# Rotary scores with a zero-padded key on all 128 rows of the array, and the latents' transposes taken up behind later steps

## The chip, the cores and the metric

The kernel runs on one core of one Trainium2 chip. The metric is the time of one execution in microseconds (us) on the device. Three runs of the kernel before gave 1155.67, 1158.75 and 1169.34 us; their median is 1158.75 us. All rows of a profile come from one further execution, which took 1158.37 us, with a span of 1156.6 us from its first to its last instruction.

The engines are named as the profile names them: PE is the matrix engine, PEld its weight loads, DVE the vector engine, ACT the scalar engine, POOL the general engine, SP the one whose queue issues nearly all transfers.

## The reference, cut to what matters

A trunk of two layers on 256 rows of width 2048 in float32. Layer 0 is a chunked gMLP. Then one shared key/value path and one attention layer with 16 heads:

```python
c_kv, k_r = jnp.split(h_kv @ w_dkv, [512], axis=-1)      # 512 latent, 64 rotary
c_kv = rms_norm(c_kv, g_kva)
kv = (c_kv @ w_ukv).reshape(B, S, 16, 128 + 128)         # key, value of each head
k_rope = apply_rope(rms_norm(k_r, g_kr), cos, sin)       # one key of 64 for all heads
c_q, z = jnp.split(h @ w_in, [512], axis=-1)
q = (rms_norm(c_q, g_qa) @ w_uq).reshape(B, S, 16, 128 + 64)
s = einsum('bqhd,bkhd->bhqk', q_nope, k_nope) + einsum('bqhr,bkr->bhqk', q_rope, k_rope)
o = softmax(causal(s * 192 ** -0.5)) @ v
x = x + gate * ((o * silu(z)) @ w_out)
```

So each score is a product over 128 values plus a product over 64 rotary values, and the rotary key is the same for all heads.

## The kernel before, in words

The 256 rows are two row tiles, t = 0 and 1, of 128. Weights come as 1 MB pieces into four raw buffers; ACT rounds a piece to `hi` (line 164), DVE makes the remainder `lo` (line 166), and every large product is three matmuls of the forms hi x hi, lo x hi, hi x lo (line 328). Small products (scores, softmax times values, transposes) are plain float32; on PE each float32 matmul of the scores stands in the trace as two.

`drive` takes a list of items one after the other. An item is one piece of weights: prepare (load and split), compute (its matmuls), post (evacuation). After each item's post, `drive` takes **one** entry from the list `later`; this list is the queue "of work that is taken up behind later steps". The attention part has the items z, y (8 each, the gate branch), d (8, the shared latent and rotary key, 576 columns as 2 x 288), c (8, the query latent, 512 columns), and then keys and queries of the head pairs in the order k k k q q k q k q k q k q k q q, each an item of 24 matmuls. A head's scores and output come from `later` once its pair is complete. Then 16 items of the output projection follow.

The order of instructions on PE, ACT, DVE and POOL is set by a scheduler when the program is built: it starts from the program's order and moves instructions by what it reckons to be ready. On the chip each engine then works strictly through its own list; a wait at its head holds everything behind it.

At the end of d the evacuation `ev_dkv` runs for t = 0 and t = 1: `latent("kv", ...)` takes the root mean square of the 512 latent columns (ACT squares, a DVE sum, a POOL power), scales them into `cn` (ACT, line 693), transposes `cn` by four PE transposes (line 697) into a PSUM bank, scales that into `hl` (DVE, line 703) and splits it into `latkv` (ACT 164, DVE 166). Then `ev_dkv` normalises the 64 rotary columns into `kn` (ACT, line 732), rotates them into `kd` (DVE), doubles them to 128 columns and transposes `kd` (line 737) into `krT` (line 738). So `krT` holds the same 64 rotary rows twice, in partitions 0 to 63 and 64 to 127. At the end of c `latent("q", ...)` does the same for the query latent into `latq`.

PSUM: the main products take four banks in turn. d holds all four (two row tiles, two halves of its columns); c needs two, which are d's banks of t = 0; the keys of pair 0 take d's other two, the keys of pair 1 take c's two.

In `scores` a head of a pair (j = 0 or 1) makes four float32 products: 128 and 256 columns of the plain part on all 128 rows (line 844), and 128 and 256 columns of the rotary part on 64 rows (line 845): `qrT` holds both heads' rotary queries, head j in partitions 64 j to 64 j + 63, and line 845 takes that half of `qrT` and of `krT`.

Of the kernel before, what the change touches and what calls it, by code (L numbers as in the profile page):

```python
# [9 lines left out]
F32 = mybir.dt.float32  # L10
# [6 lines left out]
P = 128  # L17
D = 2048
S = 256
# [4 lines left out]
DR = 64  # L24
DV = 128
R = 512
EPS = 1e-6
KD = D // P
# [21 lines left out]
BQ2 = 0.0  # L50
# [36 lines left out]
def trunk_kernel(ctx: ExitStack, tc: tile.TileContext, a: dict, out: bass.AP):  # L87
    nc = tc.nc
    ctx.enter_context(tc.manual_schedule(engines={nc.sync.engine}))
    const = ctx.enter_context(tc.tile_pool(name="const", bufs=1))  # L90
# [8 lines left out]
    def slot(name, dtype=F32):  # L99
        return big.tile([P, 2048], dtype, tag="big", name=name)  # L100

    def scratch(shape, name, tag="a", dtype=F32):
        return tmp.tile(shape, dtype, tag=tag, name=name, bufs=SCRATCH[tag])

    def bank(name, tag="aux"):
        return banks.tile(tag, name)
# [18 lines left out]
    for i in range(4):  # L125
        p = bank("pc")
# [20 lines left out]
    def rms_rstd(pieces):  # L147

        n = len(pieces)
        ss = sml.tile([P, 4], F32, tag="ss4", name="ss4")  # L150
        for i, p in enumerate(pieces):
            squares(ss[:, i:i + 1], p, "a")
        return rstd_sum(ss, n, sum(p.shape[-1] for p in pieces))
# [9 lines left out]
    def split(src, hi, lo):  # L163
        nc.scalar.copy(hi, src)  # L164
        with behind(chain.pop(0) if chain and queue[0] else None):
            nc.vector.tensor_tensor(out=lo, in0=src, in1=hi.bitcast(F32), op=ALU.subtract)  # L166
# [5 lines left out]
    hold, queue, chain = [None], [False], []  # L172
# [159 lines left out]
    later = deque()  # L332
# [315 lines left out]
    def rope(dst, src, w, t, nh):  # L648
        c = at["rc"][:, w, t:t + 1, :].broadcast_to([P, nh, DR])
        s = at["rs"][:, w, t:t + 1, :].broadcast_to([P, nh, DR])  # L650
        m = scratch([P, nh, DR], "rm", "rm")
        nc.vector.tensor_tensor(out=m, in0=src, in1=s, op=ALU.mult)
        nc.vector.tensor_tensor(out=dst, in0=src, in1=c, op=ALU.mult)
        nc.vector.tensor_tensor(out=dst[:, :, 0:32], in0=dst[:, :, 0:32], in1=m[:, :, 32:64], op=ALU.subtract)
        nc.vector.tensor_tensor(out=dst[:, :, 32:64], in0=dst[:, :, 32:64], in1=m[:, :, 0:32], op=ALU.add)

    rinv = const.tile([P, NT, 16], F32, name="rinv")
    krT = const.tile([P, S], F32, name="krT")
    lat, szb, yb = {}, {}, {}
    gate1 = Gate("ga1")  # L660
    w_b = a["b_w_in"]
# [21 lines left out]
    def lhs_h1(kk):  # L683
        return lambda c, w: at["h"].at(w, 2 * kk + c)

    def latent(which, t, pieces, gname):

        r = rms_rstd(pieces)
        cn = scratch([P, R], "cn")
        o = 0  # L690
        for p in pieces:
            n = p.shape[-1]
            nc.scalar.activation(cn[:, o:o + n], p, AF.Identity, scale=r)
            o += n
        p = bank("px", "tr")
        for j in range(4):
            nc.tensor.transpose(p[:, j * P:(j + 1) * P], cn[:, j * P:(j + 1) * P], ident)
        if which not in lat:
            lat[which] = slot("lat" + which, F32R).rearrange("p (w k t) -> p w k t", w=2, t=S)
        lt = lat[which]  # L700
        h = scratch([P, 4, P], "hl")
        for j in range(4):
            nc.vector.tensor_scalar_mul(h[:, j, :], p[:, j * P:(j + 1) * P], col[gname][:, j:j + 1])
        split(h, lt[:, 0, :, t * P:(t + 1) * P], lt[:, 1, :, t * P:(t + 1) * P])

    def z_block(i):
        def ev(t, n, ps):
            if i not in szb:
                szb[i] = slot(f"szb{i}").rearrange("p (t n) -> p t n", t=NT)
            nc.scalar.activation(piece(szb[i], t, n), ps, AF.Silu)  # L710
        return Block(lhs_h1, w_b[:, R + i * NB:R + (i + 1) * NB], KD // 2, [512, 512], ev)
# [9 lines left out]
    half = {}  # L721

    def ev_dkv(t, n, ps):
        if n == 0:
            half[t] = ps
            return
        w = R - 288
        latent("kv", t, [half[t], ps[:, 0:w]], "kva")
        kr = ps[:, w:w + DR]
        r = rms_rstd([kr])  # L730
        kn = scratch([P, 1, DR], "kn")
        nc.scalar.activation(kn[:, 0, :], kr, AF.Identity, scale=r)  # L732
        kd = scratch([P, 2, DR], "kd")
        rope(kd[:, 0:1, :], kn, 1, t, 1)
        nc.vector.tensor_copy(kd[:, 1, :], kd[:, 0, :])
        p = bank("px", "tr")
        nc.tensor.transpose(p[:, :P], kd.rearrange("p a b -> p (a b)"), ident)
        hold[0] = nc.vector.tensor_copy(krT[:, t * P:(t + 1) * P], p[:, :P])

    def lhs_lat(which):  # L740
        return lambda c, w: lat[which][:, w, c, :]
# [22 lines left out]
    def keys(i):  # L764
        def prep():
            return load_split(a["kv_w_ukv"][:, i * 512:(i + 1) * 512], 0, 512, 4)

        def comp(wt):
            pair(i)["pk"] = [bank("pk", "mm") for _ in range(NT)]
            for t in range(NT):  # L770
                mms([pairs[i]["pk"][t]], t, lhs_lat("kv"), wt, [512], True, True)

        def post():
            kT, vv = pairs[i]["kT"], pairs[i]["vv"]
            for t in range(NT):
                pv = pairs[i]["pk"][t].rearrange("p (h d) -> p h d", d=DN + DV)
                ss = sml.tile([P, 2], F32, tag="ss", name="ssk")
                for j in range(2):
                    squares(ss[:, j:j + 1], pv[:, j, 0:DN], scale=DN ** -0.5)
                nc.vector.tensor_copy(vv[:, t, :, :], pv[:, :, DN:])  # L780
                rn = head_rstd(ss, 2)
                kt = scratch([P, 2, DN], "kt")
                p = bank("px", "tr")
                for j in range(2):
                    nc.scalar.activation(kt[:, j, :], pv[:, j, 0:DN], AF.Identity, scale=rn[:, j:j + 1])
                    nc.tensor.transpose(p[:, j * P:(j + 1) * P], kt[:, j, :], ident)
                nc.scalar.copy(kT[:, :, t * P:(t + 1) * P], p[:, :2 * P].rearrange("p (h s) -> p h s", s=P))
            ready(i)
            bg(CQ)
        return prep, comp, post  # L790
# [39 lines left out]
    def attend(h):  # L830

        if h < 16:
            scores(h)
        if h > 0:
            output(h - 1)

    def scores(h):
        i, j = divmod(h, 2)
        kT, qT, qrT = (pairs[i][n] for n in ("kT", "qT", "qrT"))
        pS = bank("pS")  # L840
        pb = j * DR
        for t, (c0, c1) in enumerate(TQ):
            nk = c1 - c0
            nc.tensor.matmul(pS[:, c0:c1], lhsT=qT[:, j, t * P:(t + 1) * P], rhs=kT[:, j, 0:nk], start=True, stop=False)  # L844
            nc.tensor.matmul(pS[:, c0:c1], lhsT=qrT[pb:pb + DR, t * P:(t + 1) * P], rhs=krT[pb:pb + DR, 0:nk], start=False, stop=True)  # L845
        pr = scratch([P, P + S], "pr", "b")
        mx = sml.tile([P, 4], F32, tag="mx", name="mx")
        for t, (c0, c1) in enumerate(TQ):
            nc.vector.tensor_tensor_reduce(out=pr[:, c0:c1], in0=pS[:, c0:c1], in1=at["mask"][:, S - (c1 - c0):], scale=-SCALE, scalar=3.4e38, op0=ALU.add, op1=ALU.min, accum_out=mx[:, t:t + 1])
        sm = sml.tile([P, NT], F32, tag="sm", name="sm")  # L850
        for t, (c0, c1) in enumerate(TQ):
            nc.scalar.activation(pr[:, c0:c1], pr[:, c0:c1], AF.Exp, bias=mx[:, t:t + 1], scale=-1.0, accum_out=sm[:, t:t + 1])
        nc.vector.reciprocal(rinv[:, :, h], sm)
        soft[h] = pr
# [33 lines left out]
    def attention():  # L888
        b = z_block(1)
        b.first = banks.next  # L890
        parts = {
            "z": z_block(0).items(BQ, start=START), "y": b.items(BQ), "d": Block(lhs_k, a["kv_w_dkv"], KD // 2, [288, 288], ev_dkv).items(),
            "c": Block(lhs_h1, w_b[:, 0:R], KD // 2, [512], lambda t, n, ps: latent("q", t, [ps], "qa")).items(BQ2)}
        todo = {"q": [queries(i) for i in range(8)], "k": [keys(i) for i in range(8)]}
        for n in ORDER:
            if n in parts:
                yield from parts[n]
            else:
                yield todo[n].pop(0)
        for i in range(2):  # L900
            b = Block(lambda kk: lambda c, w: yb[kk // 4][w][:, (kk % 4) * 2 + c, :], a["b_w_out"][:, i * NB:(i + 1) * NB], KD // 2, [512, 512], lambda t, n, ps, i=i: ev_out(t, n, ps, i))
            yield from b.items(OQ, tail=1, before=lambda i=i: [gate1.piece(2 * i + n) for n in range(2)])

    def everything():
        yield from gmlp()
        yield from attention()
# [42 lines left out]
```

## Time and profile before

| | |
|---|---|
| Median of three runs | 1158.75 us (1155.67 to 1169.34) |
| The profiled execution | 1158.37 us, span 1156.6 us |
| PE busy | 1120.1 us, 97% of the span |
| PE weight loads busy | 919.3 us, 79% |
| DVE busy | 958.4 us, 83% |
| ACT busy | 623.3 us, 54% |
| POOL busy | 53.9 us, 5% |
| Moved from memory | 335.26 MB, 292 GB/s over the span |

PE is busy nearly all the time; its busy time is that of pipelined matmuls, so what a stretch of PE work costs is read from the starts of its instructions, or from the chain of waits, where each piece is the time from one start to the next. Places are given in us from the start of the span: d ends at about 888, c runs to about 916, the keys of pair 0 start at 916.5, the queries of pair 0 at 938.3, the first scores stand at 953.4, the last at about 1080, and the span ends at 1156.6.

### The profile page before, as it was taken

What the parts mean: (1) busy time and instruction counts of PE and PEld (TensorE: products, weight loads), DVE (VectorE), ACT (ScalarE), POOL (GpSimd) and SP (SyncE); (2) the same over time, 40 slices, a digit from 0 to 9 for tenths busy, and PEclk for the clock granted to TensorE, in tenths of its full rate; (3) what the DMA queues carried; (4) which work ended last, traced back from release to release, by engine and by line L of the source; (5) the groups of instructions that cost most, each with busy time, mean ns of one, the idle gap of its engine ahead of it and who ended that gap; (6) DMA issues with size and microseconds to landing.
All of it is one profiled execution on the core that took longest, in us unless ns stands there. A gap on an engine that the chain in (4) does not pass through costs nothing.

```text
span 1156.6 us, 14438 instructions
## 1 busy us (share of the span) xinstructions
PE 1120.1 (97%) x5148; PEld 919.3 (79%) x5148; DVE 958.4 (83%) x1389; ACT 623.3 (54%) x1150; POOL 53.9 (5%) x70
## 2 busy tenths in 40 slices
PE   7998999999999999999999989989999999999997
PEld 4777788888788888878888878868888788887886
DVE  6799999978998987897898888879876657687896
ACT  6744344456754434444445454457647688784332
POOL 0000000001210000000000000000000132120000
PEclk8999999999999999999999999989999999999999
DMA  9999888988898898989989989968986555245784
GB/s 354 350 344 344 309 316 329 339 295 299 301 350 338 320 345 317 357 308 348 361 306 339 335 293 339 326 246 328 359 297 196 200 155 165 84 163 199 259 301 188
DMA packets 80298, 338.30 MB, mean 292 GB/s; under 512 B 5729, under 2 KB 10209, under 8 KB 63457
## 3 DMA queue, kind: packets, MB, share of 16 engines
q1 hardware_dynamic: 79074, 335.29, 80.0%
q10 hardware_dynamic: 1152, 2.10, 0.6%
q8 instruction: 40, 0.66, 0.2%
q14 instruction: 32, 0.26, 0.1%
HBM read 335.26 MB, written 2.10 MB: 292 GB/s over the span
## 4 chain that ended last, share of the span: by engine, by line
PE 71%; DMA 10%; DVE 10%; issue 4%; ACT 4%; POOL 0%; SPq 0%; DVEq 0%; ACTq 0%; POOLq 0%
PE pm L328 58%; DMA araw<-in_ada_wT 4%; DVE lo L166 4%; PE pk L328 4%; PE pq L328 3%; DMA araw<-in_kv_ada_wT 3%; DVE araw L191 2%; ACT hi L164 1%; PE pS L845 1%; DMA raw<-in_a_w_in 1%; PE pS L844 1%; PE pmix L556 1%; ACT sq L145 1%; DMA lnb<-in_a_ln_b 1%; DVE v L467 1%
## 5 line engine op out<-in xcount | busy, mean ns | idle before, releaser
L164 ACT CAST hi<-raw 128x1024 fp32r<-128x1024 f32 (+2 forms) x376 | 382.2, 1029 | 403.2 <-PE pm L328 278.9
L166 DVE TENSOR_TENSOR lo<-raw,hi 128x1024 fp32r<-128x1024 f32 (+2 forms) x376 | 443.8, 1195 | 78.8 <-ACT hi L164 77.7
L191 DVE CUSTOM_DVE_ANT_0 araw<-araw,s_b,vec 128x2048 f32<-128x2048 f32 (+1 forms) x128 | 274.7, 2148 | 54.1 <-DMA araw<-in_ada_wT 33.6
L328 PE MATMUL pm<-lo,hh 128*128 128x512 f32 x768 | 251.9, 395 | 6.7 <-DVE lo L166 6.5
L328 PE MATMUL pm<-hi,hh 128*128 128x512 f32 x768 | 243.5, 394 | 6.6 <-ACT hh L290 3.5
L328 PE MATMUL pm<-hi,hl 128*128 128x512 f32 x768 | 247.9, 392 | 0.0
L328 PEld LDWEIGHTS pm<-lo,hh 128*128 128x128 f32 x768 | 143.8, 189 | 40.3 <-DVE lo L166 11.4
L328 PEld LDWEIGHTS pm<-hi,hh 128*128 128x128 f32 x768 | 145.0, 189 | 38.6 <-DVE v L467 4.1
L328 PEld LDWEIGHTS pm<-hi,hl 128*128 128x128 f32 x768 | 144.9, 189 | 30.8 <-DVE hl L291 0.3
L328 PE MATMUL pm<-lo,shi 128*128 128x512 f32 (+1 forms) x320 | 94.2, 371 | 2.3 <-DVE lo L166 2.3
L328 PE MATMUL pm<-hi,shi 128*128 128x512 f32 (+1 forms) x320 | 94.3, 374 | 0.9 <-ACT shi L164 0.9
L328 PE MATMUL pm<-hi,slo 128*128 128x512 f32 (+1 forms) x320 | 94.2, 372 | 0.0
L328 PEld LDWEIGHTS pm<-lo,shi 128*128 128x128 f32 x320 | 58.4, 188 | 12.6 <-DVE lo L166 2.7
L328 PEld LDWEIGHTS pm<-hi,shi 128*128 128x128 f32 x320 | 58.0, 188 | 11.0 <-ACT shi L164 1.3
L328 PEld LDWEIGHTS pm<-hi,slo 128*128 128x128 f32 x320 | 58.0, 188 | 10.0
L328 PE MATMUL pm<-hi,gh 128*128 128x512 f32 x160 | 52.9, 402 | 1.2 <-ACT kn L732 1.2
L328 PE MATMUL pm<-hi,gl 128*128 128x512 f32 x160 | 54.0, 400 | 0.0
L328 PE MATMUL pm<-lo,gh 128*128 128x512 f32 x160 | 53.5, 401 | 0.0
L328 PE MATMUL pk<-hi,latkv 128*128 128x512 f32 x128 | 43.9, 411 | 0.0
L328 PE MATMUL pm<-lo,ybh 128*128 128x512 f32 x128 | 43.2, 395 | 0.0
L328 PE MATMUL pm<-hi,ybl 128*128 128x512 f32 x128 | 43.0, 395 | 0.0
L328 PE MATMUL pm<-hi,ybh 128*128 128x512 f32 x128 | 42.9, 402 | 0.0
(178 smaller groups left out, 1240.4 us busy)
## 6 DMA issues: line engine op xcount, KB each, us to landing
araw<-in_ada_wT SPq DMA_DIRECT2D x96, 1024.0 KB, 6.5
raw<-in_a_w_in SPq DMA_DIRECT2D x96, 1024.0 KB, 6.6
raw<-in_a_w_out SPq DMA_DIRECT2D x32, 1024.0 KB, 7.2
araw<-in_kv_ada_wT SPq DMA_DIRECT2D x32, 1024.0 KB, 6.9
raw<-in_b_w_in SPq DMA_DIRECT2D x16, 1024.0 KB, 6.2
raw<-in_b_w_out SPq DMA_DIRECT2D x16, 1024.0 KB, 5.4
raw<-in_kv_w_ukv SPq DMA_DIRECT2D x8, 1024.0 KB, 5.6
raw<-in_b_w_uq SPq DMA_DIRECT2D x8, 768.0 KB, 4.9
```

The lines of the kernel that those rows point to most:

```text
L145: nc.scalar.activation(j, src, AF.Square, scale=scale, accum_out=dst)
L164: nc.scalar.copy(hi, src)
L166: nc.vector.tensor_tensor(out=lo, in0=src, in1=hi.bitcast(F32), op=ALU.subtract)
L191: nc.vector.tensor_tensor_reduce(out=t[:, c], in0=t[:, c], in1=s_b[:, c], scale=1.0, scalar=acc, op0=ALU.mult, op1=ALU.add, accum_out=dst)
L328: nc.tensor.matmul(ps[i][:, :widths[i]], lhsT=lt, rhs=rhs[:, offs[i]:offs[i] + widths[i]], start=(first and c == 0 and which == 0 and rhs ...
L467: nc.vector.tensor_tensor(out=p, in0=ps, in1=p, op=ALU.add)
L556: nc.tensor.matmul(pmix[:, j * 256:(j + 1) * 256], lhsT=wsh["T"][:, g, :], rhs=piece(vt[i], t, n)[:, j * 256:(j + 1) * 256], start=True, s ...
L844: nc.tensor.matmul(pS[:, c0:c1], lhsT=qT[:, j, t * P:(t + 1) * P], rhs=kT[:, j, 0:nk], start=True, stop=False)
L845: nc.tensor.matmul(pS[:, c0:c1], lhsT=qrT[pb:pb + DR, t * P:(t + 1) * P], rhs=krT[pb:pb + DR, 0:nk], start=False, stop=True)
```

## The change

Two things are changed.

**Scores.** `krT` becomes [128, 2, 256] and is set to zero on POOL at the start. Part 0 gets the rotary key in partitions 0 to 63 and keeps zeros in 64 to 127, part 1 the other way round. The rotary product takes all 128 rows of `qrT` (both heads) against part j, where the zeros remove the other head. The matmul has 128 rows instead of 64.

**Latents.** `latent` is cut in two: `latent_row` (squares, power, `cn`) still runs in the evacuation; `latent_turn` (transposes, `hl`, split) becomes an entry of `later`, as does the rotary key's rotation and transpose (`rope_key`). Before the entries of t = 0 an empty entry is put, which uses up the turn of the very item that ends. So for d: latent t = 0, key t = 0, latent t = 1, key t = 1 behind the first four items of c; for c: latent t = 0 behind the keys of pair 0, t = 1 behind the keys of pair 1. `cn` moves from the scratch buffers "a" to "b" (four each).

```diff
@@ -655,7 +655,8 @@
     rinv = const.tile([P, NT, 16], F32, name="rinv")
-    krT = const.tile([P, S], F32, name="krT")
+    krT = const.tile([P, 2, S], F32, name="krT")
+    nc.gpsimd.memset(krT, 0.0)
@@ -683,15 +684,19 @@
-    def latent(which, t, pieces, gname):
+    def latent_row(pieces):
 
         r = rms_rstd(pieces)
-        cn = scratch([P, R], "cn")
+        cn = scratch([P, R], "cn", "b")
         o = 0
         for p in pieces:
             n = p.shape[-1]
             nc.scalar.activation(cn[:, o:o + n], p, AF.Identity, scale=r)
             o += n
+        return cn
+
+    def latent_turn(which, t, cn, gname):
+
         p = bank("px", "tr")
         for j in range(4):
             nc.tensor.transpose(p[:, j * P:(j + 1) * P], cn[:, j * P:(j + 1) * P], ident)
@@ -725,17 +730,30 @@
         w = R - 288
-        latent("kv", t, [half[t], ps[:, 0:w]], "kva")
+        cn = latent_row([half[t], ps[:, 0:w]])
         kr = ps[:, w:w + DR]
         r = rms_rstd([kr])
         kn = scratch([P, 1, DR], "kn")
         nc.scalar.activation(kn[:, 0, :], kr, AF.Identity, scale=r)
+        if t == 0:
+            later.append(lambda: None)
+        later.append(lambda: latent_turn("kv", t, cn, "kva"))
+        later.append(lambda: rope_key(t, kn))
+
+    def rope_key(t, kn):
         kd = scratch([P, 2, DR], "kd")
         rope(kd[:, 0:1, :], kn, 1, t, 1)
         nc.vector.tensor_copy(kd[:, 1, :], kd[:, 0, :])
         p = bank("px", "tr")
         nc.tensor.transpose(p[:, :P], kd.rearrange("p a b -> p (a b)"), ident)
-        hold[0] = nc.vector.tensor_copy(krT[:, t * P:(t + 1) * P], p[:, :P])
+        nc.vector.tensor_copy(krT[0:DR, 0, t * P:(t + 1) * P], p[0:DR, :P])
+        hold[0] = nc.vector.tensor_copy(krT[DR:, 1, t * P:(t + 1) * P], p[DR:, :P])
+
+    def ev_q(t, n, ps):
+        cn = latent_row([ps])
+        if t == 0:
+            later.append(lambda: None)
+        later.append(lambda: latent_turn("q", t, cn, "qa"))
@@ -838,11 +856,10 @@
         pS = bank("pS")
-        pb = j * DR
         for t, (c0, c1) in enumerate(TQ):
             nk = c1 - c0
             nc.tensor.matmul(pS[:, c0:c1], lhsT=qT[:, j, t * P:(t + 1) * P], rhs=kT[:, j, 0:nk], start=True, stop=False)
-            nc.tensor.matmul(pS[:, c0:c1], lhsT=qrT[pb:pb + DR, t * P:(t + 1) * P], rhs=krT[pb:pb + DR, 0:nk], start=False, stop=True)
+            nc.tensor.matmul(pS[:, c0:c1], lhsT=qrT[:, t * P:(t + 1) * P], rhs=krT[:, j, 0:nk], start=False, stop=True)
@@ -890,7 +907,7 @@
-            "c": Block(lhs_h1, w_b[:, 0:R], KD // 2, [512], lambda t, n, ps: latent("q", t, [ps], "qa")).items(BQ2)}
+            "c": Block(lhs_h1, w_b[:, 0:R], KD // 2, [512], ev_q).items(BQ2)}
```

The scheduler makes new lists from this between the end of d and the first heads; before and after that stretch the lists are alike but for the rotary matmuls. ACT right after d, before (`cn` and `kn` read d's banks, `latkv` comes from the transposes):

```order
L693 ACTIVATE cn<-pm,rs_6984 128x288
L693 ACTIVATE cn<-pm,rs_6984 128x224
L145 ACTIVATE sq,ss_7003<-pm 128x64
L164 CAST latkv<-hl 128x4x128
L732 ACTIVATE kn<-pm,rs_7007 128x64
```

and now:

```order
L694 ACTIVATE cn<-pm,rs_6985 128x288
L694 ACTIVATE cn<-pm,rs_6985 128x224
L145 ACTIVATE sq,ss_6991<-pm 128x64
L737 ACTIVATE kn<-pm,rs_6995 128x64
L145 ACTIVATE sq,ss_7000<-pm 128x288
```

The cast of `latkv` no longer stands between `cn` and `kn`; it comes behind both row tiles' `kn`.

PE in the keys of pair 1, before, with the transposes of `cn` of the query latent's row tile 1 ahead of the matmuls of the keys' row tile 1:

```order
L328 MATMUL pk<-hi,latkv 128x512 x2
L328 MATMUL pk<-lo,latkv 128x512
L328 MATMUL pk<-hi,latkv 128x512
L697 MATMUL px<-ident,cn 128x128 x4
L328 MATMUL pk<-hi,latkv 128x512
```

and now, where the same transposes stand inside the queries of pair 0 (`pq`; the first ten of its 24 matmuls are shown here with the keys' transposes `kt` between them):

```order
L328 MATMUL pq<-hi,latq 128x384
L328 MATMUL pq<-lo,latq 128x384
L804 MATMUL px<-ident,kt 128x128
L702 MATMUL px<-ident,cn 128x128 x4
L328 MATMUL pq<-hi,latq 128x384 x2
L328 MATMUL pq<-lo,latq 128x384
L328 MATMUL pq<-hi,latq 128x384 x2
L328 MATMUL pq<-lo,latq 128x384
L328 MATMUL pq<-hi,latq 128x384 x2
```

The transposes moved from 36 matmuls ahead of the queries to the third place inside them. The row tile 1 of these queries (matmuls 13 to 24) needs `latq` of those transposes. ACT's list ahead of that `latq`, now:

```order
L164 CAST latq<-hl 128x4x128
L803 ACTIVATE kt<-pk,rs_7363 128x128 x2
L803 ACTIVATE kt<-pk,rs_7379 128x128 x2
L164 CAST hi<-raw 128x768
L145 ACTIVATE sq,ssk<-pk 128x128 x2
L805 COPY pair<-px 128x2x128
L164 CAST hi<-raw 128x768
L803 ACTIVATE kt<-pk,rs_7444 128x128 x2
L803 ACTIVATE kt<-pk,rs_7460 128x128
L805 COPY pair<-px 128x2x128
L803 ACTIVATE kt<-pk,rs_7460 128x128
L164 CAST latq<-hl 128x4x128
```

Between the casts of the two row tiles of `latq` stand the evacuation of the keys of pairs 1 and 2 and two splits of query weights.

## Rows read from the trace of the kernel before

**Rows 1.** The page's busy time of each engine: us, share of the span, instructions; and the granted clock of PE in 40 slices, in tenths.
```profile
PE 1120.1 (97%) x5148; PEld 919.3 (79%) x5148; DVE 958.4 (83%) x1389; ACT 623.3 (54%) x1150; POOL 53.9 (5%) x70
...
PEclk8999999999999999999999999989999999999999
```

**Rows 2.** Busy time of each engine in the stretch of the heads, in two parts: the keys and queries, then the output projection.
```profile
953.00:1040.00 87.00, 86.49 (x479) 72.18 (x477) 64.31 (x205) 69.93 (x279) 19.56 (x21) 1.00 0.42 141
1040.00:1083.00 43.00, 43.00 (x218) 33.00 (x217) 36.23 (x111) 19.81 (x52) 1.01 (x1) 1.00 0.58 207
```

**Rows 3.** The chain of waits from 1003 to 1017: start, us, what. One head's scores stand from 1005.22 to 1007.11; `pT` L862 are transposes of 128 columns on 128 rows, `pT` L866 is a float32 product of 128 columns on 128 rows.
```profile
1005.22 0.22 PE pS L844 x2
1005.44 0.41 PE pS L845 x2
1005.86 0.63 PE pS L844 x2
1006.49 0.63 PE pS L845 x2
1007.11 0.48 PE pT L862 x3
...
1012.92 0.22 PE pT L866 x2
...
1015.26 0.48 PE pT L862 x3
```

**Rows 4.** The chain of waits elsewhere: three transposes `pT` that follow no scores, and at 347.79 two float32 products of 256 columns on 128 rows (`pmix`, two instructions each).
```profile
998.31 0.33 PE pT L862 x3
...
347.79 0.86 PE pmix L556 x4
```

**Rows 5.** The lines of the rotary scores and of the copy of the rotary key, all over the span: engine, operation, count, ns least/median/most, first and last start, rows of the array and forms.
```profile
L845 PE MATMUL pS<-krT,pair x64: 272/374/480, 953.7 to 1079.3; 64*128 64x128 f32 x32, 64*128 64x256 f32 x32
...
L738 DVE COPY krT<-px x2: 284/288/292, 906.1 to 916.5; 128x128 f32<-128x128 f32 x2
```

**Rows 6.** For whom PE waited from 700 to the end: us in total, times, longest.
```profile
PE px L697 <- ACT cn L693: 4.2, 2, 2.3
...
PE pm L328 <- ACT kn L732: 1.2, 1, 1.2
PE px L786 <- ACT kt L785: 0.5, 1, 0.5
```

**Rows 7.** PE's instructions in order of time around its three waits of rows 6 that concern the latents: start, length, instruction, in brackets the idle time ahead and who ended it.
```profile
890.40 0.44 PE L697 MATMUL px<-ident,cn 128*128 128x128 f32 x2 [2.28 <-ACT cn L693]
890.59 0.59 PE L328 MATMUL pm<-hi,gh 128*128 128x512 f32 x1
...
899.35 0.50 PE L328 MATMUL pm<-hi,gh 128*128 128x512 f32 x1 [1.16 <-ACT kn L732]
...
927.25 0.65 PE L697 MATMUL px<-ident,cn 128*128 128x128 f32 x4 [1.87 <-ACT cn L693]
```

**Rows 8.** Busy time of each engine in short stretches behind these waits, and the granted clock (1.00 is 2.4 GHz, 0.50 is 1.2 GHz), which stands behind POOL's bracket.
```profile
890.83:894.24 3.41, 3.41 (x10) 2.63 (x9) 0.00 (x0) 0.06 (x1) 0.00 (x0) 0.50 0.95 342
...
899.40:902.80 3.40, 3.40 (x15) 2.83 (x16) 1.74 (x9) 2.41 (x8) 0.55 (x1) 1.00 0.02 5
...
928.37:931.79 3.42, 3.42 (x9) 2.66 (x9) 2.31 (x5) 1.82 (x4) 0.00 (x0) 0.50 0.34 126
```

**Rows 9.** ACT's instructions in order of time behind the end of d.
```profile
889.84 0.84 ACT L693 ACTIVATE cn<-pm,rs 128x288 f32<-128x288 f32 x2 [0.32 <-POOL rs L140]
...
898.22 0.62 ACT L164 CAST latkv<-hl 128x512 fp32r<-128x512 f32 x1 [7.34 <-DVE hl L703]
898.98 0.32 ACT L732 ACTIVATE kn<-pm,rs 128x64 f32<-128x64 f32 x1
```

**Rows 10.** ACT, then DVE, around the query latent's row tile 1.
```profile
926.50 0.69 ACT L693 ACTIVATE cn<-pm,rs 128x512 f32<-128x512 f32 x1 [0.40 <-POOL rs L140]
927.09 1.65 ACT L785 ACTIVATE kt<-pk,rs 128x128 f32<-128x128 f32 x6
929.10 0.62 ACT L164 CAST latq<-hl 128x512 fp32r<-128x512 f32 x1 [0.36 <-DVE hl L703]
...
927.94 1.13 DVE L703 TENSOR_SCALAR hl<-px,vec 128x128 f32<-128x128 f32 x4 [0.81 <-PE px L697]
929.75 0.69 DVE L166 TENSOR_TENSOR latq<-hl,latq 128x512 fp32r<-128x512 f32 x1 [0.68 <-ACT latq L164]
```

**Rows 11.** PE at the start of the queries of pair 0, and busy time of each engine from 940 to 960.
```profile
938.30 0.33 PE L328 MATMUL pq<-hi,latq 128*128 128x384 f32 x1
938.47 0.34 PE L328 MATMUL pq<-lo,latq 128*128 128x384 f32 x1
...
940.00:960.00 20.00, 20.00 (x113) 18.38 (x112) 13.40 (x35) 19.36 (x86) 6.87 (x7) 1.00 0.49 154
```

**Rows 12.** ACT in the softmax of the head of rows 3 (its transposes are the `pT` at 1015.26 there).
```profile
1007.89 0.49 ACT L852 ACTIVATE pr<-pr,mx 128x256 f32<-128x256 f32 x1
```

**Rows 13.** POOL at the start of the span, where the new zeroing joins.
```profile
0.94 0.32 POOL L637 MEMSET mask<- 128x256 f32 x1
...
9.01 0.56 POOL L140 TENSOR_TENSOR rs<-rs,nhalf 128x1 f32<-128x1 f32 x1 [7.17 <-DVE rs L139]
```

**Rows 14.** Who waited for whom from 1100 to the end, the longest in total.
```profile
ACT hi L164 <- DMA raw<-in_b_w_out: 9.0, 2, 5.0
```

## The prediction

> **What bounds the kernel now.** I read the page first: PE is busy for 97% of the span, and its granted clock is near full everywhere [rows 1]. Then the stretch in which the scores stand, by windows: from 953 to 1040 PE is busy 86.49 of 87 us, from 1040 to 1083 all 43 [rows 2]. No other engine is full there (ACT 69.93 of 87, DVE 36.23 of 43). The table of waits says the same from PE's side: between the first and the last score PE waited once, 0.5 us for `kt` [rows 6]. So in the heads PE is the bound, and time that its own instructions save is saved from the end, as long as the other engines keep up. Last I read PE's order of time where the latents are made: there it is not the bound. It stops at 888 for 2.28 us, at 898 for 1.16 us, and at 925 for 1.87 us [rows 7]. Behind the first and the third stop the granted clock is 0.50, that is 1.2 GHz instead of 2.4, for 3.41 us each: 10 and 9 matmuls stand in those stretches against 15 in an equally long one at 1.00, with transposes among them [rows 8]. Half of 3.41 is lost in each, 1.7 us. Behind the 1.16 us the granted clock stayed at 1.00, which is that row.
>
> **The scores.** One head has four products: plain 128 columns, rotary 128, plain 256, rotary 256, two instructions each. The chain of waits gives them 0.22, 0.41, 0.63 and 0.63 us, and the three transposes behind them 0.48 [rows 3], where three transposes that follow no rotary product take 0.33 [rows 4]. So the head costs 0.22 + 0.41 + 0.63 + 0.63 + (0.48 - 0.33) = 2.04 us. What would the products cost if nothing but full-height ones stood in a row? 128 columns: 0.22, as for the `pT` product [rows 3]. 256 columns: `pmix` is float32 on 128 rows by 256 columns, four instructions in 0.86, so 0.43 for two [rows 4]. That makes 0.22 + 0.22 + 0.43 + 0.43 = 1.30. Note that the plain 256 product, full-height itself, also costs 0.63 between two rotary ones: what is paid for is the change between 64 and 128 rows, four times a head, not the rotary product alone. The saving is 0.74 us a head, and for 16 heads (64 rotary instructions, 32 of either width [rows 5]: 16 heads with two products of two instructions) **11.8 us**.
>
> How much of this reaches the end? Below: half, if ACT or DVE takes over, since ACT would rise from 69.93 of 87 to about 69.93 of 80.5 (87%), and DVE from 36.23 of 43 to about 36.23 of 38.5 (94%). Above: all, since PE's inputs are early: the softmax of the head in rows 3 is done at 1008.38 [rows 12] and its transposes stand at 1015.26. I take 85%, **10.0 us**: the average slack is large, but there is one place with none (`kt`, 0.5 us) and both engines work through their lists in order.
>
> Here a rule of the Trainium skill speaks against the edit. The page "TensorE: Matmul & The Clock Gate", section "Why this matters for your kernels", says that a matmul over few rows takes as long as one over 128, and that the gain lies in letting different row groups run side by side. By it padding would save nothing, and the term would be 0 instead of 10.0. Rows 3 do not show that: equal columns, 0.63 next to 64-row neighbours, 0.43 without.
>
> **The latents behind d.** The first stop stays. c's first matmul writes d's bank of row tile 0, so it waits for `cn`'s reading of that bank, just as the transposes did: `cn`'s first half ends about 890.3 [rows 9], both stood at 890.40 and 890.59 [rows 7]. I count 0 for it and for the clock behind it. The second stop goes. PE waited for `kn`, which frees the second bank; `kn` stood on ACT behind the cast of `latkv`, and that cast waited 7.34 us for `hl` [rows 9], so for transposes that PE itself put behind a row of c's matmuls. Now `kn` follows the 64-column square directly, needs only a power on POOL (about 0.6), and is done before 893; row tile 1 of c comes several us later. **-1.16 us.** What is late next: c's weights, no row of PE waits for them; 0.
>
> **The query latent.** The third stop goes too. PE stood before the transposes of row tile 1, but the keys behind them would have waited as well, for c's bank that `cn` reads at 926.50 [rows 10]. Both are cured: the transposes stand elsewhere, and ACT's new list has the squares and `cn` of both row tiles next to each other, ahead of the keys' squares, so that the bank is free some us before the keys of pair 1 need it. **-1.87 us**, and the 1.2 GHz stretch behind it **-1.7 us**.
>
> What is added: the transposes of row tile 1 stand inside the queries of pair 0, three places in. Behind them lie `hl`, the cast and the remainder of `latq`: from the transposes at 927.25 to the cast's end at 929.72 are 2.47 us, to the remainder's end at 930.44 3.19 us [rows 10]. PE has ten matmuls of 0.17 us [rows 11], the four transposes and five of `kt` at 0.11 [rows 4], about 2.7 us, to do meanwhile. If ACT were free the wait would be 0 to 0.5. But ACT's list holds the keys' evacuation and two splits of weights ahead of that cast. Above, one wait at the head of ACT's list as in rows 9 is 7.34 us. Nothing excludes a gain of 0. I take **+1.2 us**, nearer to the low end, since rows 10 show this very chain with ACT at work, and no clock loss, as behind the 1.16 us.
>
> **Small terms at nothing.** Zeroing `krT`, 512 columns: under 0.7 us by the 0.32 of 256 columns, on POOL, which then has nothing to do until 9.01 [rows 13]. Two copies of 64 rows for one of 128: at most 0.29 more, twice [rows 5], on DVE, long before the first score; without that cover 0.6 us. The output projection's weights: ACT waits 9.0 us for them after 1100 [rows 14] while PE does not wait [rows 6]; their loads are issued as buffers come free, so all of it moves forward together. SP's list is unchanged.
>
> **Sum.** 1158.37 - 10.0 - 1.16 - 1.87 - 1.7 + 1.2 = 1144.8, **1145 us**. The profiled execution is 0.4 us below the median of the runs shown, so the same number stands for the median.
>
> **Rivals.**
> 1. *The 64-row products are not what is slow*; the accumulation into the bank is, or the rule above holds, and full height gains 0. The latents alone give 1.16 + 1.87 + 1.7 - 1.2 = 3.5: 1158.4 - 3.5 = 1154.9. For it: every head has the same pattern, so no head without 64 rows can be compared. Against it: `pmix` and `pT`. Chance 0.08.
> 2. *Another engine becomes the bound*: ACT, which is full from 940 to 960 already (19.36 of 20 [rows 11]), or DVE at 94%. Half of the heads' gain, 1158.4 - 5.9 - 3.5 = 1149.0. Chance 0.12.
> 3. *The wait moves into the queries*: 3.2 us there and 1.2 GHz behind it, 1.7, in place of 1.2: 1148.5. Chance 0.10.
> 4. *Slower.* ACT waits at the head of its list for `hl` once for each row tile of `latq`, 7.34 us each as in rows 9, with the keys' evacuation held behind it and two stretches at 1.2 GHz (3.4): 18.1 us against 14.7 gained and no 1.2, so 1161.8. It decides from 14.7 us of new PE idle. For it: the casts stand in the busiest stretch of ACT. Against it: the PE work that `hl` waits for is only a few matmuls away, where in rows 9 a long row of c's matmuls lay between. Chance 0.02.
> That the transposes are moved but nobody waited for them is covered by the first stop, which I leave in.
>
> **How the numbers follow.** My own case, 1141 to 1149, has 0.68. All priced gains in full with no new wait give 1158.4 - 11.8 - 4.7 = 1141.9; runs of one kernel differ by 2 to 3 us, so the low end is 1139. Rivals 2 and 3 lie inside up to 1152; of rival 1 the range takes the lower part: 1139 to 1154. Two per cent of 1158.75 are 23.2 us, about what a measurement of this kernel can tell from no change; the bounds are 1135.6 and 1181.9. Faster than 1135.6 needs more than all that is priced: 0.03. Slower than 1181.9 would be rival 4 several times over: 0.01. Within: 0.96.
>
> **What would show it.** In the profile after: the rotary products at 128 rows, four products of a head in 1.3 us of the chain; still 2.3 us before c with 1.2 GHz behind it, and no wait for `kn`; no wait and full clock in the keys of pair 1; a wait of about 1 us at `pq`, released by `latq`. I am wrong if a head still takes 1.8 us or more, if ACT or DVE end PE's waits between 945 and 1075 for more than 3 us in all, or if a stretch at 1.2 GHz follows the first queries.

## The result and the profile after

| | before | changed |
|---|---|---|
| median of 4 runs each | 1159.03 us (1155.67 to 1169.34) | 1145.2 us (1137.55 to 1150.9) |
| profiled execution, its span | 1158.37, 1156.6 us | 1144.97, 1143.2 us |
| PE busy | 1120.1 us, 97% | 1109.1 us, 97% |

The ratio is 0.9888, with a 95% interval of 0.985 to 0.9926: about 13 us, or 1.1%, are gained. The forecast was 1145, in a range of 1139 to 1154.

The page after, in the lines of [rows 1]: busy time of each engine in us, share of the span, instructions; then the granted clock of PE in 40 slices.

```profile
PE 1109.1 (97%) x5148; PEld 919.5 (80%) x5148; DVE 959.0 (84%) x1391; ACT 621.7 (54%) x1150; POOL 55.0 (5%) x71
...
PEclk9999999999999999999999999998999999999999
```

PE has as many instructions as before and 11.0 us less of busy time. The chain of waits shows where this comes from. One head's scores after the change, to be laid beside [rows 3]: start, us, what (L861 plain, L862 rotary, L879 the transposes behind them).

```profile
999.18 0.22 PE pS L861 x2
999.40 0.22 PE pS L862 x2
999.62 0.43 PE pS L861 x2
1000.06 0.43 PE pS L862 x2
1000.49 0.33 PE pT L879 x3
```

The four products take 0.22 + 0.22 + 0.43 + 0.43 = 1.30 us, and the transposes cost 0.33 instead of 0.48. Who PE waited for from 700 to 1156, in us in total, times and longest, to be laid beside [rows 6]:

```profile
PE pm L328 <- ACT cn L694: 2.3, 1, 2.3
...
PE px L804 <- ACT kt L803: 1.5, 1, 1.5
...
PE px L836 <- ACT qt L830: 0.3, 1, 0.3
PE pq L328 <- ACT latq L164: 0.2, 1, 0.2
```

Of the two waits for `cn` one is left, and it is c's first matmul now that waits. The wait for `kn` is gone. The wait for `kt` has grown from 0.5 to 1.5, and two small ones are new, 0.3 for `qt` and 0.2 for `latq`.

PE in order of time at three places, which answer to [rows 7] and to [rows 11] (start, length, instruction, idle time ahead and who ended it):

```profile
891.74 0.50 PE L328 MATMUL pm<-hi,gh 128*128 128x512 f32 x1 [2.28 <-ACT cn L694]
...
933.91 0.42 PE L328 MATMUL pq<-hi,latq 128*128 128x384 f32 x1
...
934.47 0.60 PE L702 MATMUL px<-ident,cn 128*128 128x128 f32 x4
...
936.78 0.96 PE L804 MATMUL px<-ident,kt 128*128 128x128 f32 x4
937.93 0.44 PE L328 MATMUL pq<-hi,latq 128*128 128x384 f32 x1 [0.18 <-ACT latq L164]
...
976.33 0.59 PE L804 MATMUL px<-ident,kt 128*128 128x128 f32 x2 [1.52 <-ACT kt L803]
```

And the windows, to be laid beside [rows 8, 11] (stretch, its length, busy time of PE, its weight loads, DVE, ACT and POOL with instructions, then the granted clock):

```profile
892.40:895.80 3.40, 3.40 (x11) 2.62 (x10) 0.55 (x4) 1.48 (x7) 1.10 (x2) 0.50 0.90 320
919.00:926.00 7.00, 7.00 (x33) 5.79 (x32) 3.91 (x8) 5.29 (x19) 1.40 (x2) 1.00 0.49 153
926.00:934.00 8.00, 8.00 (x42) 6.58 (x41) 5.14 (x13) 5.53 (x18) 2.50 (x3) 1.00 0.67 196
940.00:960.00 20.00, 19.66 (x109) 17.70 (x108) 14.89 (x43) 19.19 (x76) 8.40 (x7) 1.00 0.51 176
```

The 1.2 GHz stretch behind the first stop stands as it was. The one in the keys of pair 1 is gone: these keys now stand from 921.9 to 927.6, and the clock from 919 to 934 is 1.00.

**How the runs are compared below.** Single executions differ by several us, and the traces show where: d ends between 884.2 and 892.5 us in the eleven profiles of this study, while what follows repeats closely. So each version is also given by its stages, counted from the end of d. These are read off the starts of PE's first instruction of each stage (last row: the end of the span), as differences to the kernel before; the last column is run 8.

| from the end of d to | before, us | after | scores alone | latents alone | earlier turn | free banks | both |
|---|---|---|---|---|---|---|---|
| keys of pair 0 | 28.41 | -1.40 | 0.00 | -1.40 | -1.38 | -5.71 | -5.74 |
| keys of pair 2 (behind the keys of pairs 0 and 1) | 44.11 | -5.97 | +0.11 | -5.97 | -5.57 | -10.15 | -9.79 |
| queries of pair 1 | 54.83 | -4.15 | +0.09 | -4.16 | -5.18 | -8.36 | -9.38 |
| last score | 191.21 | -14.55 | -10.78 | -3.58 | -15.85 | -19.00 | -20.06 |
| end of span | 268.51 | -14.75 | -10.97 | -3.58 | -16.04 | -19.19 | -20.26 |

### The profile page after: what moved, and what is told of

Read it like the earlier page. It is cut to its first block, busy times and chain, and to the rows that moved or that the text cites. A ratio compares the mean times of both kernels' runs of the same rounds, so it can differ in the third digit from the quotient of the medians.

```text
span 1143.2 us, 14438 instructions
## 1 busy us (share of the span) xinstructions
PE 1109.1 (97%) x5148; PEld 919.5 (80%) x5148; DVE 959.0 (84%) x1391; ACT 621.7 (54%) x1150; POOL 55.0 (5%) x71
## 4 chain that ended last, share of the span: by engine, by line
PE 72%; DVE 11%; DMA 9%; issue 4%; ACT 3%; POOL 0%; SPq 0%; DVEq 0%; ACTq 0%; POOLq 0%
PE pm L328 60%; DMA araw<-in_ada_wT 5%; DVE lo L166 4%; PE pk L328 4%; DVE araw L191 3%; PE pq L328 2%; DMA raw<-in_a_w_in 1%; DMA araw<-in_kv_ada_wT 1%; ACT hi L164 1%; ACT sq L145 1%; PE pmix L556 1%; PE pS L861 1%; PE pS L862 1%; DMA lnb<-in_a_ln_b 1%; DVE v L467 1%
```

## The experiments

Nine runs were made, in three groups, each group beside the kernel before on one chip. Runs 7 and 8 are one kernel, and run 9 is the changed kernel itself. All compute the same output.

**1. The scores alone.** The kernel before with the zero-padded key and nothing else:

```diff
-    krT = const.tile([P, S], F32, name="krT")
+    krT = const.tile([P, 2, S], F32, name="krT")
+    nc.gpsimd.memset(krT, 0.0)
...
-            nc.tensor.matmul(pS[:, c0:c1], lhsT=qrT[pb:pb + DR, t * P:(t + 1) * P], rhs=krT[pb:pb + DR, 0:nk], start=False, stop=True)
+            nc.tensor.matmul(pS[:, c0:c1], lhsT=qrT[:, t * P:(t + 1) * P], rhs=krT[:, j, 0:nk], start=False, stop=True)
```

> The kernel before with the zero-padded key alone; the latents are turned in place as before. Theory (the two parts are separate, PE bounds the heads): a head's four products go from 2.04 to 1.30 us in the chain of waits; between the first score and the last PE gains some 10.4 us, what the changed kernel gained there, and the time falls by about 10.5 us against the kernel before; the three stops of PE at the latents (2.3, 1.2, 1.9 us) stay. Rival (the heads gain only because the latents' part gave the other engines a lead): the heads gain 8 us or less and ACT or DVE end waits of PE there.

Measured: 1147.95 us, ratio 0.9918 (0.9887 to 0.9948); behind the end of d 10.97 us less, nearly all of it (10.87) between the queries of pair 1 and the last score. PE's waits, in the form used above:

```profile
PE px L698 <- ACT cn L694: 4.2, 2, 2.3
...
PE px L788 <- ACT kt L787: 1.2, 1, 1.2
PE pm L328 <- ACT kn L733: 1.2, 1, 1.2
```

The stops of the latents are all still there, and the wait for `kt` has grown without the latents being touched. So faster heads cause it: counted from the end of d, PE arrives at this place 2.95 us sooner than before and ACT's `kt` is ready only 2.23 sooner. These 0.7 are most of the 0.9 by which 10.87 falls short of 11.8.

**2. The latents alone.** The changed kernel with line 845 of before:

```diff
-            nc.tensor.matmul(pS[:, c0:c1], lhsT=qrT[:, t * P:(t + 1) * P], rhs=krT[:, j, 0:nk], start=False, stop=True)
+            nc.tensor.matmul(pS[:, c0:c1], lhsT=qrT[pb:pb + DR, t * P:(t + 1) * P], rhs=krT[pb:pb + DR, 0:nk], start=False, stop=True)
```

> The changed kernel with the 64-row rotary products of before; only the latents' transposes are handed on. Theory: the stretch from the end of d to the second queries is shorter than before by about 4.2 us, as in the changed kernel, a head costs 2.04 us, and the time falls by about 4 us against the kernel before. Rival (the new wait at the queries grows when the heads leave PE less room): 2 us or less.

Measured: 1154.04 us, ratio 0.9967 (0.994 to 0.9994); 3.58 us less behind the end of d. The two parts together make 10.97 + 3.58 = 14.55, against 14.75 for the whole change: they add up, and neither needs the other. Of the 4.16 gained up to the queries of pair 1, 0.6 go again behind them: there PE waits 0.79 for `kt` instead of 0.51, and 0.34 for `qt`, which it did not wait for before.

**3. What is slow, the 64-row product or the change of height?** Rotary products on 64 rows again, but in the order plain 128, rotary 128, rotary 256, plain 256, so that a head changes height twice instead of four times:

```diff
+            for part in ((0, 1), (1, 0))[t]:
+                if part == 0:
+                    nc.tensor.matmul(pS[:, c0:c1], lhsT=qT[:, j, t * P:(t + 1) * P], rhs=kT[:, j, 0:nk], start=t == 0, stop=t == 1)
+                else:
+                    nc.tensor.matmul(pS[:, c0:c1], lhsT=qrT[pb:pb + DR, t * P:(t + 1) * P], rhs=krT[pb:pb + DR, 0:nk], start=t == 1, stop=t == 0)
```

> The kernel of the run with the latents alone, rotary products on 64 rows, but each head's four products in the order plain 128, rotary 128, rotary 256, plain 256: PE changes between 128 and 64 rows twice a head instead of four times; the work is the same. Theory (the change of height costs, 0.74 us a head for four changes, so 0.185 each): a head goes from 2.04 to 1.67 us, and from the end of d to the end of the span 264.9 us become about 260. Rival (products on 64 rows are slow by themselves): the head stays at 2.04 and the stretch at 264.9.

Measured: 1149.66 us, ratio 0.9937 (0.9913 to 0.9962); 259.73 us from the end of d to the end of the span, 8.8 less than before and 5.2 less than with four changes a head (experiment 2, 264.93). One head in its chain of waits (L862 plain, L864 rotary, L881 the transposes):

```profile
1000.61 0.22 PE pS L862 x2
1000.83 0.85 PE pS L864 x4
1001.68 0.63 PE pS L862 x2
1002.31 0.33 PE pT L881 x3
```

The rotary products of both widths take 0.85 together, which is 0.22 + 0.43 and one change of 0.2. The plain 256 product behind them takes 0.63, which is 0.43 and the other change. The transposes, now behind a full-height product, are back at 0.33 with 64-row products still in the head. So a head costs 1.70, and two changes cost 0.40 over the 1.30 of full height. Before, four changes cost 0.74. The single records show the 64-row products among themselves: from the second of the four rotary instructions to the third pass 0.11 us, from the third to the fourth 0.22, as between full-height ones of 128 and of 256 columns. So the 64-row product as such costs what a full one does; the change is what is paid for.

**4. The two heads of a pair side by side.** Rotary products on 64 rows, both heads of a pair together in two banks, the products of head 0 (partitions 0 to 63) and head 1 (64 to 127) in turn:

```diff
+        if j == 0:
+            both[:] = [bank("pS"), bank("pS")]
+            for t, (c0, c1) in enumerate(TQ):
+                for part in ((0, 1), (1, 0))[t]:
+                    for b in range(2):
...
+                            nc.tensor.matmul(both[b][:, c0:c1], lhsT=qrT[pb:pb + DR, t * P:(t + 1) * P], rhs=krT[pb:pb + DR, 0:c1 - c0], start=t == 1, stop=t == 0)
```

> As the run with two changes a head, but both heads of a pair are scored together in two banks: two plain products, the two rotary products of 128 columns (one head on rows 0 to 63, the other on rows 64 to 127), the two of 256, two plain ones. Two changes of height a pair instead of eight. Theory (only changes cost, 0.185 each, and row groups do not run side by side): a pair's products cost 2.6 + 0.37 = 2.97 us instead of 4.08, and from the end of d to the end some 257 us. Rival (the Trainium skill's rule: row groups run side by side): the two rotary products of a pair take the time of one, the pair 2.97 - 0.65 = 2.3 us, less than the 2.6 of the changed kernel, and the stretch is about 252, below the 253.8 of the changed kernel.

Measured: 1150.81 us, ratio 0.9935 (0.9907 to 0.9963); 259.67 us behind the end of d, not 252 and not 257. One pair in its chain of waits (L864 plain, L866 rotary):

```profile
1003.74 0.45 PE pS L864 x4
1004.18 0.86 PE pS L866 x8
1005.04 1.06 PE pS L864 x4
```

The eight rotary instructions take 0.86 us, where at full height they take 2 x (0.22 + 0.43) = 1.30. Less a change of 0.2 this is 0.66, half of 1.30: the two row groups ran side by side, and the records of their instructions start 7 ns apart. That is the rule of the Trainium skill weighed in the prediction (the page "TensorE: Matmul & The Clock Gate", section "Why this matters for your kernels"), and on this point the trace agrees. The pair takes 2.37 us against 2.60 for two heads of the changed kernel. On the matmuls of this pair the rival was right, on the time nobody was. PE's waits are one reason:

```profile
PE pm L328 <- ACT ybh L164: 1.3, 1, 1.3
PE pT L887 <- DVE pts L886: 1.2, 2, 1.0
PE px L802 <- ACT kt L801: 0.7, 1, 0.7
PE pm L328 <- ACT qt L829: 0.4, 1, 0.4
PE px L834 <- ACT qt L828: 0.3, 1, 0.3
```

These five rows are 3.9 us (1.3 of them, for `ybh`, behind the last score), against 0.5 before and 1.9 in the changed kernel. The larger reason is that the built list splits pairs: it has 30 changes of height where 16 were meant, and only 14 of the 32 couples of rotary instructions start within 7 ns of each other. In four of the eight pairs the heads stand apart altogether, each with two changes as in experiment 3:

```profile
1053.85 0.85 PE pS L866 x4
```

Estimated from these numbers, 14 more changes at 0.2 are 2.8 us, four pairs without the overlap 4 x 0.65 = 2.6, and the longer waits 2.0: 7.4 of the 7.7 us by which the stretch is above 252. Whether a list without these splits would beat full height was not tried.

**5. The turn of the query latent.** The changed kernel without the empty entry for the query latent, so that its transposes come one item earlier:

```diff
     def ev_q(t, n, ps):
         cn = latent_row([ps])
-        if t == 0:
-            later.append(lambda: None)
         later.append(lambda: latent_turn("q", t, cn, "qa"))
```

> The changed kernel without the empty entry ahead of the query latent's turns: row tile 0 is turned at the end of c, row tile 1 behind the keys of pair 0, one step earlier. Theory (the 1.6 us that the first queries lost come from the transposes and the cast of latq standing inside them): the first queries take 4.7 us again instead of 6.2, no stop comes in the keys of pair 1 since ACT still does both cn ahead, and the time falls by 1 to 1.5 us against the changed kernel. Rival (ACT's own backlog of keys holds the queries): the first queries take 6 us as before and nothing is gained; second rival: the stop in the keys of pair 1 comes back, 1.9 us and 1.2 GHz behind it.

Measured: 1140.64 us, ratio 0.986 (0.9827 to 0.9892); 1.29 us less than the changed kernel behind the end of d. The queries of pair 0 take 4.73 us, as before (4.65), where the changed kernel takes 6.22. No stop returns in the keys: between c's first matmul and the heads the table of waits has none for PE. So the empty entry was not needed against the third stop; it only cost time. But the transposes of row tile 1 have not come back to where they stood before: they are at 928.41, in the keys of pair 2, one stage behind the place of the old stop. `cn` of both row tiles is done at 916.93, ahead of either place.

**6. The first stop.** The changed kernel with c in banks that d does not hold. A phase of banks is put in ahead of the last one: from y up to the end of c the main products take six banks in turn and two are left for the rest; with the first keys it is four and four again.

```diff
-BANKS = ({"mb": 2, "aux": 2}, {"mb": 1, "aux": 3}, {"aux": 4})
+BANKS = ({"mb": 2, "aux": 2}, {"mb": 1, "aux": 3}, {"mb": 2, "aux": 2}, {"aux": 4})
...
+            if i == 0:
+                banks.next()
```

> The changed kernel with six banks in turn for the main products up to the end of c (two for the rest), and four again from the keys on; c then finds banks that d does not hold. Theory (the first stop, 2.28 us ahead of c, is the wait for d's bank alone): the stop goes, the 1.2 GHz behind it goes too, and the time from the end of d to the keys of pair 0 falls by about 4 us, the time by about 4 us against the changed kernel. Rival (c would wait for something else, or two banks for transposes are too few): the stop moves to another place between the end of d and the keys, and less than 2 us is gained.

Measured: 1138.35 us, ratio 0.9842 (0.9814 to 0.987); 4.44 us less than the changed kernel behind the end of d. The stretch behind c's first matmul in windows, to be laid beside the first window of the changed kernel above:

```profile
885.90:889.30 3.40, 3.40 (x16) 2.81 (x15) 2.56 (x4) 3.29 (x7) 0.65 (x2) 1.00 0.88 299
```

16 matmuls stand in 3.40 us at 1.00, where the changed kernel has 11 at 0.50. The stop of 2.28 us came from the bank alone, and the 1.2 GHz came with the stop. c's first matmul starts 0.07 us behind the end of d instead of 2.28; these 2.2 and 3.4 / 2 = 1.7 of the clock make 3.9 of the 4.3 us by which the keys of pair 0 start sooner.

**7 and 8. Both edits.** 5 and 6 together, run twice:

> The changed kernel with both cures: six banks in turn up to the end of c, and the query latent turned one step earlier. Theory (they cure two separate waits): from the end of d to the end 253.8 - 4.45 - 1.3 = 248 us, and the time about 1.6% below the kernel before. Rival (with c's start earlier ACT has less lead in the keys, so the second cure is lost there): 249.3 as with the banks alone.

Measured: 1138.98 us, ratio 0.9845 (0.9796 to 0.9894), with one execution of six at 3942.81 (the other five have a median of 1136.3); 248.23 us behind the end of d. Since that interval is wide, the same kernel ran again:

> The kernel with both cures once more, since one execution of its first series lay far off. Theory: 248 us from the end of d to the end again, the time 1.6 to 2.0% below the kernel before and about 5.5 us below the changed kernel. Rival (the last 1.1 us over the banks alone were chance): 249.3 from the end of d.

Measured: 1134.34 us (1133.54 to 1135.43, six runs), ratio 0.9789 (0.9761 to 0.9817); 248.25 us behind the end of d. From the end of d on PE has one wait left, in the form used above:

```profile
PE px L804 <- ACT kt L803: 1.2, 1, 1.2
```

This version is faster than both kernels: by 24.6 us than the one before on the same chip, and by 8.6 than the changed kernel there (run 9, 1142.93). Behind the end of d it gains 268.51 - 248.25 = 20.3 over the kernel before and 5.5 over the changed one. The rest of either difference is not traced. In the profiled executions it lies ahead of the end of d, where two profiles of the changed kernel alone differ by 2.5 us (889.46 and 887.01); the edit of the banks reaches y and d too, and from its first matmul to its end d takes 25.48 us in runs 6 to 8, where the changed kernel takes 25.70.

**9. The changed kernel again**, beside 8:

> The changed kernel itself on the same chip, to set it beside both cures and to see how far it repeats. Theory (what lies behind the end of d repeats, what lies ahead of it varies): 253.8 us from the end of d to the end again within 0.3, while the end of d itself lies anywhere from 884 to 893; the time about 1.1% below the kernel before. Rival (the gain depends on the execution): the stretch differs by a us or more.

Measured: 1142.93 us, ratio 0.9872 (0.9837 to 0.9906); 253.78 us behind the end of d, where the first profile had 253.76.

## Why the prediction was right, point by point

**The bound.** PE was the bound in the heads: what its instructions saved came off the end (experiment 1).

**The scores, -10.0.** A head takes 1.30 in the chain, as worked out from `pT` and `pmix`, so 11.8 was the sum in full. From the queries of pair 1 to the last score the change gained 14.55 - 4.15 = 10.4 us, 88% where 85% were taken. What is missing, 1.4 us: PE waits 1.52 for `kt` instead of 0.51, and 0.34 at 947.87 for `qt`, ahead of the first scores, where it did not wait before. The one place named as having no slack is where most of it went. The reading that the change of height is paid for, not the 64-row product, was shown by experiment 3.

**The rule against it.** The rule of the Trainium skill (the page "TensorE: Matmul & The Clock Gate", section "Why this matters for your kernels") that few rows take as long as 128 holds as it stands (experiment 3: 64-row products behind each other cost what full ones do, 0.11 and 0.22 us an instruction). The result which the prediction drew from it, a term of 0, does not follow: it leaves out what a change of height costs.

**The first stop, 0.** It stayed, at 2.28, with 1.2 GHz behind it, because c's first matmul needs d's bank. Experiment 6 gave c other banks and both went.

**The second stop, -1.16.** It went, by the way given. ACT's list after the change, in order of time (start, length, instruction, idle time ahead and who ended it):

```profile
891.19 0.84 ACT L694 ACTIVATE cn<-pm,rs 128x288 f32<-128x288 f32 x2 [0.32 <-POOL rs L140]
...
893.14 0.31 ACT L737 ACTIVATE kn<-pm,rs 128x64 f32<-128x64 f32 x1 [0.92 <-POOL rs L140]
...
899.39 0.62 ACT L164 CAST latkv<-hl 128x512 fp32r<-128x512 f32 x1 [1.68 <-DVE hl L708]
```

`kn` ends at 893.45, 4.0 us behind the end of d (889.46), where before it ended 11.2 behind it (899.30 [rows 9], 888.12), and the cast stands behind it. The keys of pair 0 start 1.40 sooner: these 1.16 and 0.24 more. Most of that is how a stop is counted: the matmuls ahead of it start 0.23 us apart but last 0.39 by the record, and the idle time begins at the end of the last one, so each stop took 0.16 more than its idle time. The two transposes that stood ahead of c gave nothing; they stand inside c now and cost as much there.

**The third stop and its clock, -1.87 and -1.7.** Both went. From the keys of pair 0 to those of pair 2 5.97 - 1.40 = 4.57 us were gained, 1.0 more than the 3.57 of the sum. About 0.8 of this are eight transposes, 0.11 each [rows 4], which only moved: four of row tile 1, and four of row tile 0, which stood at 922.01 and now stand at 928.87; 0.16 more is the stop's, as above. The clock was sized well: the twelve matmuls of 512 columns (and two transposes) in which its 3.41 us stood took 4.57 us and take 2.98 now, 1.6 less where 1.7 was summed. The sum named two cures, and no run parts them: in experiment 5 the transposes stand elsewhere too. By the times the order of ACT's list would have done it alone: `cn` of row tile 1 ends at 919.45, where before it ended at 927.19, and the matmuls that followed the old stop start at 924.63.

**The new wait, +1.2.** The size was about right (the queries of pair 0 took 1.58 longer; 0.44 of it are the four transposes that came in and 0.22 two more of `kt`, which leaves 0.9), its form was not. The prediction looked for 1 us at `pq`, released by `latq`; the row shows 0.18 there. The larger part stands just ahead: from 936.78 to the `pq` at 937.93 pass 1.15 us, those 0.18 among them, for four transposes of `kt` that cost 0.44 elsewhere. ACT hands out their `kt` late: it splits weights and scales `kt` in the same stretch of its list, and the cast of `latq` (937.25) comes behind them. So the cover was late itself, as the prediction feared of ACT's list, and nearly hid the wait that was looked for: with `kt` on time PE would have stood at this `pq` from 937.2 on, and the cast ends at 937.88.

**The sum.** Behind the end of d the sum was 1158.37 - 1144.8 = 13.6 us, measured 14.75. That the profiled execution agrees to 0.2 us has luck in it: its end of d came 1.3 us later than in the execution before. The spread of single executions was taken too small, 2 to 3 us: the three of the kernel before that were known differ by 13.7 (1155.67 to 1169.34), and of the four of the changed kernel one, 1137.55, lies under the low end of 1139. The median lies within.

**The rivals.** The second (ACT or DVE the bound) did not come: from 945 to 1075 PE waited 1.5 us for `kt` and 0.3 for `qt`, under the 3 us named. The third did not: the clock is 1.00 from 926 to 934 and from 940 to 960. The fourth did not: ACT does not idle ahead of `latq`'s casts (931.82 and 937.25), so nothing is held up by them. The first falls with experiment 1, though half of its premise, that the 64-row product is not slow, holds (experiment 3).

**Terms at nothing.** POOL zeroed `krT` in 0.528 us at 0.9 and each pair of copies took 0.28 + 0.29 on DVE at 905 and 914, with the first score at 948.

## What to carry to other kernels

When small-height matmuls stand between full ones, count the changes of height, not the small products: pad to full height, or order them so that equal heights stand together, and read the price off the full-height neighbour in the chain. When an engine stops at the seam of two stages, ask which bank and which place in the other engine's list it waits for: here the moved work went with a better list on ACT, moving it a step further than needed cost 1.3 us, and two more banks in turn were worth 4.4.

## What the runs showed of the hardware that was not expected

- Each change between 128 and 64 rows cost about 0.2 us (0.74 for four, 0.40 for two). By the single records it is shared: from the last instruction ahead of it to the first behind it pass 0.20 us and from that one to the next 0.21, where two of 128 columns at one height are 0.11 apart. So a full-height product beside it looks slow (0.63 for 0.43 [rows 3]). What in the change takes the time, no run shows.
- Two 64-row float32 products in different halves of the rows, into different banks, ran side by side: 0.66 us for what takes 1.30 one after the other (experiment 4).
- Whether the clock falls does not follow from the length of a stop alone. One stop, for a `lo` of DVE ahead of the attention, stands in every profile: behind 2.29 us of it (before, at 690.81) the granted clock stayed at 1.00, behind 1.94 us (scores alone, at 689.25) it was 0.50. Behind 1.52 us at 976.33 of the changed kernel it was 1.00 too. The windows, in this order:

```profile
691.00:694.40 3.40, 3.40 (x16) 2.79 (x16) 3.40 (x4) 1.87 (x3) 0.00 (x0) 1.00 0.78 300
...
689.70:693.10 3.40, 3.40 (x10) 2.61 (x9) 3.40 (x4) 0.97 (x3) 0.00 (x0) 0.50 0.83 316
...
976.90:980.30 3.40, 3.40 (x20) 2.88 (x19) 1.02 (x5) 3.40 (x18) 0.00 (x0) 1.00 0.31 111
```

So the clock's part of a stop is less sure than the stop. Behind the first stop it came in all eight profiles that have this stop, behind the third in both.

- What varies most from run to run lies ahead of the end of d (884.2 to 892.5 us in the eleven profiles). Behind it the same kernel repeated to 0.02 us in two pairs of runs (253.76 and 253.78; 248.23 and 248.25), so a term of half a us can be read there that medians of whole runs would not show.
